# A running log-sum-exp along time: three time steps per partition instead of two, Exp written over its input, and one load split over two queues

## The chip, the cores and the metric

The kernel runs on one core of a Trainium2 chip. The metric is device time in microseconds (us). Before the change it is 1265.37 us, the median of 10 runs (1264.45 to 1265.74). The engines named below are PE (TensorE, matrix multiply), ACT (ScalarE, functions of one element), DVE (VectorE), POOL (GpSimd) and SP (SyncE, which here only issues transfers). DMA stands for the 16 engines that move data between the chip's memory and the core's buffer.

## What is computed

The input x has shape 4 x 4096 x 4128 (batch, time, feature), float32. Along time the output is the running log-sum-exp:

```python
out[:, 0, :] = x[:, 0, :]
for t in range(1, S):
    mx = np.maximum(out[:, t - 1, :], x[:, t, :])
    out[:, t, :] = mx + np.log(np.exp(out[:, t - 1, :] - mx) + np.exp(x[:, t, :] - mx))
```

The same as the logarithm of a running sum of exp(x). The kernel computes it in that form: exponential, prefix sum, logarithm. Input and output are 270.5 MB each, and each is moved once.

## The kernel before

A tile is 256 time steps of one batch: 128 partitions with R = 2 consecutive time steps each, 4128 features wide. One partition's part of a transfer is thus one run of 2 x 4128 x 4 = 33,024 bytes. There are 16 tiles per batch, 64 in all. Each is loaded into a buffer of the pool `xpool` (5 buffers), overwritten there with the result, and stored from there.

The features are cut into four chunks of 1024; the last has the 32 left-over features added. For each chunk:

- `exp` (L107, its instruction at L111) has ACT write exp(x) of both time steps, as fp16, into a buffer of a second pool, `epool` (4 buffers).
- `head` (L114) has PE add up in a PSUM buffer: a triangle of ones (`incl`) times the first time step, a strict triangle (`excl`) times the second, and `pick` times the carry. That is the running sum at each partition's first time step. There are three such PSUM buffers, used in turn. The carry of each chunk is the sum at the end of the tile before, in two fp16 parts.
- `ln(0, c)` (L125, L126) has ACT write the logarithm over x.
- `second` (L128) adds the second time step with an identity matrix, so that the buffer holds the sum at each partition's second time step.
- `close` (L133) takes the logarithm of that, and `keep` (L88) has DVE copy the last partitions into the carry with two instructions (L90, L91).

The 32 left-over features have a PSUM buffer of their own (`tail_mm`, L138) and one Ln for both time steps (L149).

The order is written out by hand (`manual_schedule`, L83), and every engine executes its instructions in that order. In `run` (L155) the chunks of one tile overlap: while chunk c is exponentiated, chunk c-1 takes its first Ln and chunk c-2 its second. At the end of a tile the chunks in flight are finished before the next tile's first Exp.

SP issues all transfers from one queue (L102 loads, L153 stores). Four loads are issued at the start; from then on the load of tile i+3 (L183) is issued ahead of tile i's work and store, and it waits until the store that last used its buffer, that of tile i-2, is done. A store waits for the last Ln of its tile, and everything behind it in SP's queue waits with it.

Of the kernel before, what the change touches and what calls it, by code (L numbers as in the profile page):

```python
# [7 lines left out]
FP32 = mybir.dt.float32  # L8
FP16 = mybir.dt.float16
ACT = mybir.ActivationFunctionType  # L10
P = 128
R = 2
CH = 1024
MM = 512
HI, LO = 96, 32
# [2 lines left out]
def _constants(nc, pool):  # L18


    def tri(base, name):
        t = pool.tile([P, P], FP16, name=name)
        nc.gpsimd.memset(t, 1.0)

        nc.gpsimd.affine_select(  # L25
            out=t, in_=t, pattern=[[1, P]], compare_op=mybir.AluOpType.is_ge,
            fill=0.0, base=base, channel_multiplier=-1,
        )
        return t

    def ones_where_zero(bases, step, name):
        t = pool.tile([P, P], FP16, name=name)
        nc.gpsimd.memset(t, 0.0)
        for base in bases:
            nc.gpsimd.affine_select(  # L35
                out=t, in_=t, pattern=[[step, P]], compare_op=mybir.AluOpType.not_equal,
                fill=1.0, base=base, channel_multiplier=1,
            )
        return t

    return (
        tri(0, "incl"),
        tri(-1, "excl"),
        ones_where_zero([0], -1, "ident"),
        ones_where_zero([-(HI + 31), -(LO + 31)], 0, "pick"),
    )


@with_exitstack
def kernel(  # L50
    ctx: ExitStack,
    tc: tile.TileContext,
    x: bass.AP,
    out: bass.AP,
):

    nc = tc.nc
    B, S, D = x.shape  # L60
    rows = P * R
    n_t = S // rows
    assert S % rows == 0
    n_main = D // CH
    tail = D - n_main * CH
    t0 = n_main * CH

    nc.scalar.preload_act_table_set("natural_log_exp_and_others")  # L68
    consts = ctx.enter_context(tc.tile_pool(name="consts", bufs=1))
    incl, excl, ident, pick = _constants(nc, consts)  # L70

    xpool = ctx.enter_context(tc.tile_pool(name="xpool", bufs=5))
    epool = ctx.enter_context(tc.tile_pool(name="epool", bufs=4))
    cpool = ctx.enter_context(tc.tile_pool(name="cpool", bufs=1))
    pmain = ctx.enter_context(tc.tile_pool(name="pmain", bufs=3, space=bass.MemoryType.PSUM))
    ptail = ctx.enter_context(tc.tile_pool(name="ptail", bufs=2, space=bass.MemoryType.PSUM))

    carry = [cpool.tile([P, CH], FP16, name=f"carry{c}") for c in range(n_main)]
    carry_t = cpool.tile([P, tail], FP16, name="carry_t")
    for t in (*carry, carry_t):  # L80
        nc.vector.memset(t, 0.0)  # L81

    ctx.enter_context(tc.manual_schedule())  # L83

    def mm(pt, w, rhs, start, stop):
        nc.tensor.matmul(pt, lhsT=w, rhs=rhs, start=start, stop=stop, skip_group_check=True)  # L86

    def keep(cr, pt):  # L88

        nc.vector.tensor_copy(cr[HI:HI + 32, :], pt[HI:HI + 32])  # L90
        nc.vector.tensor_tensor(  # L91
            out=cr[LO:LO + 32, :], in0=pt[HI:HI + 32], in1=cr[HI:HI + 32, :],
            op=mybir.AluOpType.subtract,
        )

    class Step:
        def __init__(self, b, k):
            self.first = k == 0
            self.xt = xpool.tile([P, R, D], FP32, name="xt")
            self.et, self.pt = {}, {}  # L100
            self.dram = lambda t: t[b, k * rows:(k + 1) * rows, :].rearrange("(p j) d -> p j d", j=R)
            nc.sync.dma_start(out=self.xt, in_=self.dram(x))  # L102

        def cols(self, c):
            return slice(c * CH, (c + 1) * CH if c + 1 < n_main else D)

        def exp(self, c):  # L107
            s = self.cols(c)
            w = s.stop - s.start
            et = epool.tile([P, R, CH + tail], FP16, name="et")  # L110
            nc.scalar.activation(et[:, :, :w], self.xt[:, :, s], ACT.Exp)  # L111
            self.et[c] = et

        def head(self, c):  # L114
            et = self.et[c]
            pt = self.pt[c] = pmain.tile([P, CH], FP32, name="pt")
            for s in range(0, CH, MM):
                mm(pt[:, s:s + MM], incl, et[:, 0, s:s + MM], True, False)
            for s in range(0, CH, MM):
                mm(pt[:, s:s + MM], excl, et[:, 1, s:s + MM], False, self.first)  # L120
            if not self.first:
                for s in range(0, CH, MM):
                    mm(pt[:, s:s + MM], pick, carry[c][:, s:s + MM], False, True)

        def ln(self, j, c):  # L125
            nc.scalar.activation(self.xt[:, j, c * CH:(c + 1) * CH], self.pt[c], ACT.Ln)  # L126

        def second(self, c):  # L128
            pt = self.pt[c]
            for s in range(0, CH, MM):  # L130
                mm(pt[:, s:s + MM], ident, self.et[c][:, 1, s:s + MM], False, True)

        def close(self, c):  # L133

            self.ln(1, c)
            keep(carry[c], self.pt[c])

        def tail_mm(self):  # L138
            et = self.et[n_main - 1]
            qt = self.qt = ptail.tile([P, R, tail], FP32, name="qt")  # L140
            e0, e1 = et[:, 0, CH:], et[:, 1, CH:]
            for j in range(R):
                mm(qt[:, j, :], incl, e0, j == 0, False)
                mm(qt[:, j, :], incl if j else excl, e1, False, self.first)
                if not self.first:
                    mm(qt[:, j, :], pick, carry_t, False, True)

        def ln_tail(self):
            nc.scalar.activation(self.xt[:, :, t0:D], self.qt, ACT.Ln)  # L149
            keep(carry_t, self.qt[:, 1, :])  # L150

        def store(self):
            nc.sync.dma_start(out=self.dram(out), in_=self.xt)  # L153

        def run(self):  # L155
            last = n_main - 1
            self.exp(0)
            self.head(0)
            for c in range(1, n_main):
                self.exp(c)  # L160
                self.head(c)
                if c == last:
                    self.tail_mm()
                self.ln(0, c - 1)
                self.second(c - 1)
                if c >= 2:
                    self.close(c - 2)
            self.ln(0, last)
            self.second(last)
            self.close(last - 1)  # L170
            self.ln_tail()
            self.close(last)
            self.store()

    work = [(b, k) for b in range(B) for k in range(n_t)]
    ahead = 3
    steps = []
    for i, (b, k) in enumerate(work):
        if i == 0:
            steps += [Step(*work[n]) for n in range(ahead)]  # L180
        if i + ahead < len(work):
            n = i + ahead
            steps.append(Step(*work[n]))  # L183
        steps[i].run()


# [28 lines left out]
```

The softmax here doesn't subtract the row's maximum and nothing guards it: scores larger than these inputs give would overflow.

## Time and profile before

| | |
|---|---|
| median of 10 runs | 1265.37 us |
| the profiled execution's own time | 1265.42 us |
| its span, first to last instruction | 1263.6 us |
| moved over the span | 541.5 MB, 428 GB/s to and from memory |
| ACT busy: Exp (L111) | 485.5 us in 256 instructions |
| ACT busy: Ln (L126) | 504.6 us in 512 instructions |
| DVE busy: carry (L90 and L91) | 314.8 and 314.0 us in 256 each |
| PE: 512-column matmuls | 505 ns mean with `incl` or `excl`, 427 ns with `ident` |
| loads, issue to landing | 64 of 4128 KB, median 29.4 us |
| stores, issue to landing | 64 of 4128 KB, median 38.7 us |

In a group's row, the numbers after the bar are its busy time, the mean duration of one in ns, and the idle time of the engine just ahead of it with what ended that idle time. A row of waits has who waited, for whom, and then the total in us, how often, and the longest. In a row of the timeline come the start, the time until the end of the last of the instructions merged in it, the engine and line, and how many there are.

### The profile page before, as it was taken

What the parts mean: (1) busy time and instruction counts of PE and PEld (TensorE: products, weight loads), DVE (VectorE), ACT (ScalarE), POOL (GpSimd) and SP (SyncE); (2) the same over time, 40 slices, a digit from 0 to 9 for tenths busy, and PEclk for the clock granted to TensorE, in tenths of its full rate; (3) what the DMA queues carried; (4) which work ended last, traced back from release to release, by engine and by line L of the source; (5) the groups of instructions that cost most, each with busy time, mean ns of one, the idle gap of its engine ahead of it and who ended that gap; (6) DMA issues with size and microseconds to landing.
All of it is one profiled execution on the core that took longest, in us unless ns stands there. A gap on an engine that the chain in (4) does not pass through costs nothing.

```text
span 1263.6 us, 7025 instructions
## 1 busy us (share of the span) xinstructions
PE 663.3 (52%) x2392; PEld 242.7 (19%) x2392; DVE 655.7 (52%) x645; ACT 962.9 (76%) x833; POOL 2.2 (0%) x13
## 2 busy tenths in 40 slices
PE   2565655545545565464554645546445464554651
PEld 1222222111112121121121211212112121121210
DVE  3565565464454544645546455464564544545443
ACT  6889878778778787786877877778778787787872
POOL 0000000000000000000000000000000000000000
PEclk9878878767687677877767777777777777767776
DMA  9999999999999999999999999999999999999997
GB/s 401 418 431 431 432 430 431 432 429 432 432 435 433 432 430 433 432 434 430 433 434 433 431 432 432 433 432 433 434 434 434 433 428 432 432 434 432 434 433 330
DMA packets 18466, 541.51 MB, mean 429 GB/s; under 512 B 2048, under 2 KB 2048, under 8 KB 2048
## 3 DMA queue, kind: packets, MB, share of 16 engines
q1 hardware_dynamic: 18432, 541.07, 99.5%
q8 instruction: 19, 0.31, 0.1%
q14 instruction: 15, 0.12, 0.0%
HBM read 270.53 MB, written 270.53 MB: 428 GB/s over the span
## 4 chain that ended last, share of the span: by engine, by line
DMA 81%; ACT 2%; PE 1%; SPq 1%; DVE 1%; issue 0%; ACTq 0%
DMA out_dram<-xt 77%; DMA xt<-in_x_dram 5%; ACT et L111 1%; ACT xt L126 1%; PE pt L86 1%; SPq L102 1%; DVE carry L90 0%; DVE carry L91 0%; SPq L153 0%; DVE carry_t L90 0%; DVE carry_t L91 0%; ACTq L126 0%
## 5 line engine op out<-in xcount | busy, mean ns | idle before, releaser
L90 DVE CAST carry<-pt 32x1024 f16<-32x1024 f32 x256 | 314.8, 1230 | 575.0 <-ACT xt L126 571.8
L111 ACT ACTIVATE et<-xt 128x2048 f16<-128x2048 f32 (+1 forms) x256 | 485.5, 1921 | 153.3 <-DMA xt<-in_x_dram 153.3
L126 ACT ACTIVATE xt<-pt 128x1024 f32<-128x1024 f32 x512 | 504.6, 1029 | 123.4 <-PE pt L86 62.6
L86 PE MATMUL pt<-et,incl 128*128 128x512 f16 x512 | 211.1, 505 | 548.5 <-ACT et L111 379.6
L91 DVE TENSOR_TENSOR carry<-pt,carry 32x1024 f16<-32x1024 f32 x256 | 314.0, 1226 | 8.8
L86 PE MATMUL pt<-et,excl 128*128 128x512 f16 x512 | 211.5, 505 | 0.0
L86 PEld LDWEIGHTS <-incl 128*128 128x128 f16 x704 | 69.2, 111 | 683.1 <-issue 631.6
L86 PE MATMUL pt<-carry,pick 128*128 128x512 f16 x480 | 195.2, 498 | 0.0
L86 PE MATMUL pt<-et,ident 128*128 128x512 f16 x512 | 174.5, 427 | 27.3 <-ACT xt L126 27.3
L86 PEld LDWEIGHTS <-excl 128*128 128x128 f16 x576 | 71.2, 124 | 115.8 <-issue 83.3
L86 PEld LDWEIGHTS <-pick 128*128 128x128 f16 x600 | 69.8, 119 | 94.8 <-issue 66.7
L86 PEld LDWEIGHTS <-ident 128*128 128x128 f16 x512 | 49.5, 106 | 102.1 <-issue 76.2
L86 PE MATMUL qt<-et,incl 128*128 128x32 f16 x192 | 19.6, 189 | 0.0
L86 PE MATMUL qt<-carry_t,pick 128*128 128x32 f16 x120 | 15.6, 182 | 0.0
L149 ACT ACTIVATE xt<-qt 128x64 f32<-128x64 f32 x64 | 14.5, 227 | 0.0
L90 DVE CAST carry_t<-qt 32x32 f16<-32x32 f32 x64 | 12.6, 196 | 2.0
L91 DVE TENSOR_TENSOR carry_t<-qt,carry_t 32x32 f16<-32x32 f32 x64 | 12.4, 193 | 2.2
L86 PE MATMUL qt<-et,excl 128*128 128x32 f16 x64 | 11.6, 182 | 0.0
L81 DVE MEMSET carry<- 128x512 uint32 x4 | 1.9, 485 | 1.1 <-PEq L199 1.0
L68 ACT ACT_TABLE_LOAD x1 | 1.3, 1283 | 0.8 <-PEq L199 0.8
L35 POOL TENSOR_SCALAR_AFFINE_SELECT pick<-pick 128x128 f16<-128x128 f16 x2 | 0.6, 298 | 0.1
L25 POOL TENSOR_SCALAR_AFFINE_SELECT incl<-incl 128x128 f16<-128x128 f16 x1 | 0.3, 298 | 0.0
(11 smaller groups left out, 1.9 us busy)
## 6 DMA issues: line engine op xcount, KB each, us to landing
xt<-in_x_dram SPq DMA_DIRECT2D x64, 4128.0 KB, 29.4
out_dram<-xt SPq DMA_DIRECT2D x64, 4128.0 KB, 38.7
```

The source lines that it names most:

```text
L25: nc.gpsimd.affine_select(out=t, in_=t, pattern=[[1, P]], compare_op=mybir.AluOpType.is_ge, fill=0.0, base=base, channel_multiplier=-1,)
L35: nc.gpsimd.affine_select(out=t, in_=t, pattern=[[step, P]], compare_op=mybir.AluOpType.not_equal, fill=1.0, base=base, channel_multiplier=1,)
L68: nc.scalar.preload_act_table_set("natural_log_exp_and_others")
L81: nc.vector.memset(t, 0.0)
L86: nc.tensor.matmul(pt, lhsT=w, rhs=rhs, start=start, stop=stop, skip_group_check=True)
L90: nc.vector.tensor_copy(cr[HI:HI + 32, :], pt[HI:HI + 32])
L91: nc.vector.tensor_tensor(out=cr[LO:LO + 32, :], in0=pt[HI:HI + 32], in1=cr[HI:HI + 32, :], op=mybir.AluOpType.subtract,)
L102: nc.sync.dma_start(out=self.xt, in_=self.dram(x))
L111: nc.scalar.activation(et[:, :, :w], self.xt[:, :, s], ACT.Exp)
L126: nc.scalar.activation(self.xt[:, j, c * CH:(c + 1) * CH], self.pt[c], ACT.Ln)
L149: nc.scalar.activation(self.xt[:, :, t0:D], self.qt, ACT.Ln)
```

## The change

Rows: R is 3. A tile is 384 time steps, three per partition, so that one run is 49,536 bytes. 4096 steps are 32 x 128, which makes ten tiles of three and one of two per batch, 44 tiles in all. In the first batch the tile of two comes first, in the others last.

Buffers: Exp writes fp16 into the first half of the bytes of its own x columns (a view of the same buffer as fp16). `epool` is gone; `xpool` has four buffers of three rows.

Order: the work is cut into chunks with stages. `head` adds the first time step with `incl` and all others with `excl`. `stage(j)` takes the Ln of time step j, then adds step j+1 with the identity; after the last step it keeps the carry. In each round of a tile the stages of three chunks are emitted, the oldest first, then the Exp two chunks on and the `head` one chunk on. A tile's chunks are finished before the next tile begins. The tail's matmuls read the same columns several times over by a broadcast view.

Transfers: three loads are issued at the start. After that each tile's store is issued at its end and then the load three tiles on. That load uses the buffer of the tile before, and so waits for the store before. One load, issued after the 23rd tile, is split: 80 partitions on SP, 45 on POOL, 3 on SP, with a small load into `pad` on POOL before and after.

```diff
-R = 2
+R = 3
...
-    xpool = ctx.enter_context(tc.tile_pool(name="xpool", bufs=5))
-    epool = ctx.enter_context(tc.tile_pool(name="epool", bufs=4))
+    bufs = 4
+    xpool = ctx.enter_context(tc.tile_pool(name="xpool", bufs=bufs))
...
+        def load(self, split=False):
+            full = xpool.tile([P, R, D], FP32, name="xt")
+            self.xt = full[:, :self.r, :]
+            self.half = self.xt.bitcast(FP16)
+            if not split:
+                nc.sync.dma_start(out=self.xt, in_=self.dram(x))
+                return
...
+            pad = cpool.tile([12, 16], FP32, name="pad")
+            nc.gpsimd.dma_start(out=pad[:5, :], in_=x[0, :5, :16])
+            nc.sync.dma_start(out=self.xt[:80], in_=self.dram(x)[:80])
+            nc.gpsimd.dma_start(out=self.xt[80:125], in_=self.dram(x)[80:125])
+            nc.sync.dma_start(out=self.xt[125:], in_=self.dram(x)[125:])
+            nc.gpsimd.dma_start(out=pad, in_=x[0, :12, :16])
...
+        def e(self, j, a, b):
+            return self.t.half[:, j, 2 * self.c * CH + a:2 * self.c * CH + b]
...
+        def exp(self):
+            c0, w = self.c * CH, self.w
+            nc.scalar.activation(
+                self.t.half[:, :, 2 * c0:2 * c0 + w], self.t.xt[:, :, c0:c0 + w], ACT.Exp,
+            )
...
+        def head(self):
+            t = self.t
+            pt = self.pt = pmain.tile([P, CH], FP32, name="pt")
+            for j in range(t.r):
+                for s in range(0, CH, MM):
+                    mm(pt[:, s:s + MM], excl if j else incl, self.e(j, s, s + MM), start=j == 0)
+            if not t.first:
+                for s in range(0, CH, MM):
+                    mm(pt[:, s:s + MM], pick, carry[self.c][:, s:s + MM])
+            if self.c == last:
+                self.tail_head()
...
+            for i in range(r):
+                e = self.e(i, CH, CH + tail)
+                mm(qt[:, i:, :], incl, to(e, r - i), start=i == 0)
+                if i:
+                    mm(qt[:, :i, :], excl, to(e, i))
+            if not t.first:
+                mm(qt, pick, to(carry_t, r))
...
+        def stage(self, j):
...
+            t, c, pt = self.t, self.c, self.pt
+            nc.scalar.activation(t.xt[:, j, c * CH:(c + 1) * CH], pt, ACT.Ln)
+            if j + 1 < t.r:
+                for s in range(0, CH, MM):
+                    mm(pt[:, s:s + MM], ident, self.e(j + 1, s, s + MM), stop=j + 2 == t.r)
+                if c == last and j == 0:
+                    nc.scalar.activation(t.xt[:, :, t0:D], self.qt, ACT.Ln)
+                    keep(carry_t, self.qt[:, t.r - 1, :])
+            else:
+                keep(carry[c], pt)
...
+    ahead = bufs - 1
+    for s in steps[:ahead]:
+        s.load()
+    for n, s in enumerate(steps):
+        chunks = [Chunk(s, c) for c in range(n_main)]
+        chunks[0].exp()
+        chunks[1].exp()
+        chunks[0].head()
+        for g in range(n_main + s.r - 1):
+            for d in range(s.r - 1, -1, -1):
+                if 0 <= g - d < n_main:
+                    chunks[g - d].stage(d)
+            if g + 2 < n_main:
+                chunks[g + 2].exp()
+            if g + 1 < n_main:
+                chunks[g + 1].head()
+        s.store()
+        if n + ahead < len(steps):
+            steps[n + ahead].load(split=n == len(steps) // 2)
```

## The prediction

> **What bounds the kernel now.** I read the page first: engine totals, the DMA slices, the queues, the chain that ended last.
>
> ```profile
> PE 663.3 (52%) x2392; PEld 242.7 (19%) x2392; DVE 655.7 (52%) x645; ACT 962.9 (76%) x833; POOL 2.2 (0%) x13
> ...
> DMA  9999999999999999999999999999999999999997
> ...
> DMA packets 18466, 541.51 MB, mean 429 GB/s; under 512 B 2048, under 2 KB 2048, under 8 KB 2048
> ...
> q1 hardware_dynamic: 18432, 541.07, 99.5%
> ...
> DMA 81%; ACT 2%; PE 1%; SPq 1%; DVE 1%; issue 0%; ACTq 0%
> ```
>
> One queue keeps the 16 DMA engines busy for 99.5% of the span; ACT, the busiest engine, has 76%. Then SP's waits: the load of L102 waits for an older store, that is for DMA itself, not for compute.
>
> ```profile
> SPq L102 <- DMA out_dram<-xt: 1083.8, 59, 19.5
> ```
>
> Next, stretches of the end (columns: window, length, PE, PEld, DVE, ACT, POOL, clock, DMA share, GB/s).
>
> ```profile
> 1250.00:1253.00 3.00, 0.00 (x0) 0.00 (x0) 0.00 (x0) 0.00 (x0) 0.00 (x0) 0.50 0.94 407
> 1253.00:1255.00 2.00, 0.00 (x0) 0.00 (x0) 0.00 (x0) 0.00 (x0) 0.00 (x0) 0.50 0.80 347
> 1255.00:1257.00 2.00, 0.00 (x0) 0.00 (x0) 0.00 (x0) 0.00 (x0) 0.00 (x0) 0.50 0.42 182
> 1257.00:1259.00 2.00, 0.00 (x0) 0.00 (x0) 0.00 (x0) 0.00 (x0) 0.00 (x0) 0.50 0.23 99
> 1259.00:1261.00 2.00, 0.00 (x0) 0.00 (x0) 0.00 (x0) 0.00 (x0) 0.00 (x0) 0.50 0.08 33
> ```
>
> The engines do not stop together: by 1258 under a quarter of them still work. The landing records of the last store say the same: first engine at 1253.8, fifteenth at 1261.0, last at 1262.75. So the time is the amount of transfer of the slowest engine. Last, the ACT side, since a change of its order could make it the bound: groups by shape, and one tile that did not wait for its load.
>
> ```profile
> L126 ACT ACTIVATE xt<-pt 128x1024 f32<-128x1024 f32 x512 | 504.6, 1029 | 123.4 <-PE pt L86 62.6 <-issue 59.4 <-ACT et L111 0.6
> L111 ACT ACTIVATE et<-xt 128x2048 f16<-128x2048 f32 x192 | 359.3, 1904 | 153.3 <-DMA xt<-in_x_dram 153.3
> ```
>
> ```profile
> 28.50 3.73 ACT L111 ACTIVATE et<-xt 128x2048 f16<-128x2048 f32 x2
> 33.30 1.02 ACT L126 ACTIVATE xt<-pt 128x1024 f32<-128x1024 f32 x1 [1.07 <-PE pt L86]
> ...
> 36.02 1.93 ACT L126 ACTIVATE xt<-pt 128x1024 f32<-128x1024 f32 x2
> ...
> 42.17 1.94 ACT L126 ACTIVATE xt<-pt 128x1024 f32<-128x1024 f32 x2 [0.54 <-PE pt L86]
> ...
> 45.01 3.73 ACT L111 ACTIVATE et<-xt 128x2048 f16<-128x2048 f32 x2
> ```
>
> Such a tile took 45.01 - 28.50 = 16.5 us; DMA needs 8.454 MB / 433 GB/s (steady rate in the windows) = 19.5 us for its load and store. ACT waits the rest: 153.3 us for loads. Two Ln in 1.93 us instead of 2 x 1.02 show that neighbours overlap by 0.11.
>
> [...]
>
> **The change, part by part.**
>
> Bytes: unchanged, 541 MB. Below that DMA time cannot fall, so the gain is at most what packets and unevenness cost.
>
> Longer runs. A packet of 33,024 B took 1.222 us (median of the trace's packet records), one of 8,192 B (instructions) 0.309. The line through both is 27.2 B/ns and 7.8 ns per packet[...]. A packet of 49,536 B is then 7.8 + 1821.2 = 1829 ns, not shown by the trace. One engine moves 8 packets of each transfer: before 128 x 8 = 1024 x 1.222 = 1251.3 us, and 128 semaphore packets of 9 ns, 1.2. After: 40 tiles of three rows and 4 of two, 88 loads and stores: 640 x 1.829 + 64 x 1.222 = 1248.8, and some 92 x 9 ns = 0.8. Gain 2.9 us. Bounds: 0, if a run this long is served as several packets; 320 x 13 ns = 4.2, if all of 99.5% x 16 x 1263.6 / 16,384 = 1.228 us over the 1.214 that 27.2 B/ns needs were paid per packet. I take 2.9, as two sizes lie on one line.
>
> Split load (step 25: 80 rows on SP, 45 on POOL, 3 on SP). [...] If the spared engine is the one that lands last (1262.75), the next decides, 1260.99: gain 1.8. If it is another: 0, or 1.8 lost when one of the three was last. I take 1.5 of gain. The POOL queue holds nothing else by then; SP issues two pieces, 0.33 to 0.43 us each in the timeline, where a queue of tens of us stands behind it (store to landing 38.7 us median).
>
> Exp and the pools. [...] so 3 x 2.75 + 2.83 + 12 x 1.03 (Ln) + 0.25 (tail) = 23.7 us of ACT for three rows, less 17 overlaps of 0.11: 21.9. Matmuls per row stay 4 x 512 columns and chunk half; carry copies fall from 256 to 176 pairs of 2.46 us. In-place writing removes the fp16 pool; I cost it at nothing.
>
> Drain per tile. The stalls that this order leaves on ACT: (a) at the start, Exp 0 (2.75), eight cold matmuls (0.43 each, 3.4) and their end and signal, 0.36: first Ln at 6.5, Exp 1 issued out by 5.3: 1.2. (b) The matmuls of chunk 3 need chunk 0's PSUM buffer: third Ln of chunk 0 ends at 15.7, two carry copies 2.5, signal 0.1, eight warm matmuls 8 x 0.215 + 0.3: ready 20.3, ACT free 19.2: 1.1. (c) At the end the last Ln waits for two identity matmuls, 0.8. Sum 3.1: one tile 25.0 us; with all matmuls cold the same walk gives 28.8. The DMA period of a tile is 16 x 1.829 = 29.3 us. So ACT is covered, by 4.3 us or, all cold, by 0.5. Sum over the kernel: 40 x 25 + 4 x 18 = 1072 us of ACT under 1250 of DMA.
>
> Four buffers, load behind store. Load 3 is no longer issued at once but after store 0. DMA has loads 0 to 2 until 1.8 + 9.8 + 2 x 14.7 = 41 us; store 0 is out at 13.3 (landing of load 0 now) + 18 = 31: cover 10 us. Then store 1 at 56 against 65. Later the queue holds a load and a store, 29 us, when SP waits for store n-1: no gap. At the end, load 43 landing at 0: DMA has store 41 until 14.7; tile 42's compute ends near 5.5, so store 42 follows until 29.4; tile 43 ends at 24.5. Covered too.
>
> Sum on the profiled execution: 1263.6 - 2.9 - 1.5 = 1259.2 us of span; the run around it was 1265.42, 1.8 more, and equals the median 1265.37. Forecast 1261.0.
>
> **The rivals.**
> 1. No gain: long runs cost what they did and the spared engine was not the last. 1265.4 - 0.3 (semaphores) to + 1.8: about 1265. For it: which engine is last is not in any view. Against: two packet sizes on one line. 0.15.
> 2. Slower, ACT: x, Exp and result now share a buffer that matmuls read. If each wait is taken per buffer, not per column range, every Ln stands behind the matmuls issued before it and every group of matmuls behind the Exp before it. The same walk in strict turns gives 37 us for a three-row tile, 25 for a two-row one: 13 + 40 x 37 + 4 x 25 + 10 = 1603. It decides from 29.3 us per tile, 4.3 over my walk; each us beyond costs 40. For it: nothing in this trace shows two engines on parts of one buffer at once. Against: the parts are disjoint. 0.12.
> 3. Slower, DMA: the longer run is served less well; 1% on 80 large transfers is 640 x 18 ns = 11.7 us, 1261 + 11.7 = 1273. For it: no run of that length in the trace. Against: 8 KB and 33 KB have one rate. 0.12.
> 4. More gain: the engines also drift apart less with fewer packets. The mean engine is idle for 12% of the last 63.6 us, 7.6, of which some 3 more could go: 1257. 0.05.
>
> **How the numbers follow.** Forecast 0.56, its own range 1258.5 to 1263.5 (packet cost 0 to 4.2, relief 0 to 1.8). About 0.2%, 2.5 us, is what a measurement of this kernel can tell from no change, so the line is 1262.8. Of the forecast 0.51 lies below and 0.05 within; rival 4 adds 0.05 faster, rival 1 0.02 faster and 0.13 within; rivals 2 and 3 0.24 slower. Faster 0.58, same 0.18, slower 0.24. The range runs 1257.0 to 1269.0: it takes in the forecast, rivals 1 and 4 and the lower part of 3.
>
> **What would show it.** Right: hardware queue near 99.5% again, about 11,300 large packets, GB/s 433 or 434 in the middle slices, ACT still waiting for loads (by about 29.3 - 25 = 4 us a tile), last windows that fall off more steeply. Wrong: ACT waiting for PE in every tile with SP's store waiting for ACT and DMA digits under 9 (rival 2); 433 falling with DMA digits at 9 (rival 3); a gap between 31 and 65 us (buffers); the same staircase at the end (rival 1).

## The result, and the profile after

The changed kernel takes 1288.35 us (median of 8 runs, 1286.31 to 1290.43), beside 1265.42 for the kernel before in the same comparison: ratio 1.0182, 95% interval 1.0173 to 1.0190. It is 23 us slower where 4 us of gain were forecast. The profiled execution took 1288.76 us, with a span of 1287.0.

The page of the changed kernel, first the DMA rows in 40 slices of 32.2 us, then its queues:

```profile
DMA  9999999999999999999999999999999999999997
GB/s 402 427 429 430 436 426 438 425 435 439 425 439 432 431 440 425 435 431 437 428 368 302 308 430 435 433 432 437 429 436 433 434 429 437 429 437 434 427 429 321
DMA packets 12788, 541.47 MB, mean 421 GB/s; under 512 B 1494, under 2 KB 1494, under 8 KB 1494
...
q1 hardware_dynamic: 12630, 538.84, 98.2%
q0 software_dynamic: 128, 2.23, 1.1%
```

The digit of busy DMA is 9 in all slices but the last, as before. The row under it is the one to read: three slices in the middle moved 368, 302 and 308 GB/s, and the others about what they moved before. Against 433 the three lack (65 + 131 + 125) x 32.2 / 433 = 23.9 us. The whole loss sits in one place, and there the DMA engines are busy but slow. Queue q0 is POOL's; its 128 packets are those of the split load and its two small ones, and nothing else uses it.

Windows of 10 us over that place (columns as in the prediction; the last three are PE clock, DMA share and GB/s; a packet counts whole in the window where it starts, so a share can pass 1):

```profile
660.00:670.00 10.00, 7.08 (x22) 2.64 (x22) 0.00 (x0) 9.22 (x7) 1.02 (x2) 0.75 1.26 391
670.00:680.00 10.00, 6.00 (x24) 2.15 (x23) 6.50 (x7) 6.89 (x9) 0.00 (x0) 0.83 0.91 163
680.00:690.00 10.00, 0.33 (x2) 0.00 (x0) 3.71 (x4) 1.02 (x1) 0.00 (x0) 0.60 0.94 183
690.00:700.00 10.00, 0.00 (x0) 0.10 (x1) 0.00 (x0) 1.39 (x1) 0.00 (x0) 0.50 0.92 367
700.00:710.00 10.00, 7.46 (x19) 2.60 (x19) 0.00 (x0) 8.84 (x5) 0.00 (x0) 0.53 1.07 413
710.00:720.00 10.00, 6.74 (x23) 2.40 (x22) 4.80 (x4) 8.55 (x7) 0.00 (x0) 0.83 1.00 228
720.00:730.00 10.00, 2.23 (x14) 0.77 (x12) 5.42 (x7) 4.13 (x5) 0.00 (x0) 0.82 0.92 248
```

There are two dips. The pieces of the split load are issued at 663; POOL's queue is empty, so its 45 rows start 4 us later (first packet at 667.5), while the 80 rows on SP stand behind some 40 us of earlier work: 67.6 us from issue to landing, beside 31.8 for POOL's rows. The first dip, 660 to 700, lacks (42 + 270 + 250 + 66) x 10 / 433 = 14.5 us; the second, 700 to 730, lacks 9.5. The packet records name the cause more closely: packets of 49,536 B took 1.829 us almost everywhere, but POOL's 45 took 3.5 to 6.2 us each. SP's whole transfers beside them were slow too, most of their packets at 2.9 to 5 us, and in the second dip the slow packets took mostly 3.5 to 4. PE, DVE and ACT have almost nothing to do from 690 to 698.6, because ACT waits 17.2 us for a load there.

### The profile page after: what moved, and what is told of

It reads as the page before. It is cut to its first block, busy times and chain, and to the rows that moved or that the text cites. A ratio compares the mean times of both kernels' runs of the same rounds, so it can differ in the third digit from the quotient of the medians.

```text
span 1287.0 us, 6175 instructions
## 1 busy us (share of the span) xinstructions
PE 682.8 (53%) x2268; PEld 244.0 (19%) x2268; DVE 451.4 (35%) x445; ACT 977.1 (76%) x733; POOL 3.9 (0%) x16
## 4 chain that ended last, share of the span: by engine, by line
DMA 56%; ACT 21%; PE 18%; issue 2%; another core or an unknown queue 1%; DVE 0%; ACTq 0%; SPq 0%
DMA xt<-in_x_dram 32%; DMA out_dram<-xt 24%; PE pt L87 18%; ACT xt L171 12%; ACT xt L137 9%; ACT xt L176 0%; DVE carry L91 0%; DVE carry L92 0%; PE qt L87 0%; ACTq L237 0%; ACTq L137 0%; SPq L113 0%
## 5 line engine op out<-in xcount | busy, mean ns | idle before, releaser
L137 ACT ACTIVATE xt<-xt 128x3072 f16<-128x3072 f32 (+3 forms) x176 | 475.3, 2701 | 103.6 <-DMA xt<-in_x_dram 102.2
L91 DVE CAST carry<-pt 32x1024 f16<-32x1024 f32 x176 | 216.4, 1230 | 721.6 <-ACT xt L171 716.8
L87 PE MATMUL pt<-xt,ident 128*128 128x512 f16 x672 | 235.3, 437 | 315.0 <-ACT xt L171 314.4
L87 PE MATMUL pt<-xt,incl 128*128 128x512 f16 x352 | 156.3, 539 | 269.4 <-ACT xt L137 268.9
L87 PE MATMUL pt<-xt,excl 128*128 128x512 f16 x672 | 259.7, 526 | 0.0
L92 DVE TENSOR_TENSOR carry<-pt,carry 32x1024 f16<-32x1024 f32 x176 | 215.9, 1226 | 6.1
L87 PEld LDWEIGHTS <-excl 128*128 128x128 f16 x756 | 94.5, 127 | 148.6 <-issue 120.4
L87 PE MATMUL pt<-carry,pick 128*128 128x512 f16 x320 | 119.6, 462 | 0.0
L87 PEld LDWEIGHTS <-incl 128*128 128x128 f16 x480 | 51.5, 111 | 356.3 <-issue 305.5
L87 PEld LDWEIGHTS <-pick 128*128 128x128 f16 x360 | 42.3, 117 | 64.0 <-issue 46.9
## 6 DMA issues: line engine op xcount, KB each, us to landing
xt<-in_x_dram SPq DMA_DIRECT2D x1, 3870.0 KB, 67.6
xt<-in_x_dram POOLq DMA_DIRECT2D x1, 2176.9 KB, 31.8
```

Source lines behind the costliest of these rows:

```text
L92: nc.vector.tensor_tensor(out=cr[LO:LO + 32, :], in0=pt[HI:HI + 32], in1=cr[HI:HI + 32, :], op=mybir.AluOpType.subtract,)
L137: nc.scalar.activation(self.t.half[:, :, 2 * c0:2 * c0 + w], self.t.xt[:, :, c0:c0 + w], ACT.Exp,)
```

## The experiments

Three theories stood at the start. P: the pieces themselves are slow, because each covers only some of the partitions, so that their packets take a multiple. Why they should be slow no trace or run of this case shows. Q: what costs is POOL's queue, whose transfer takes turns with SP's: in the trace of the changed kernel POOL's packets begin in three rounds of 15, at 667.5, 676.8 and 685.2, with 18 and 16 packets of SP begun between the starts of the rounds. R: the tiles of three rows, the four buffers or the drain cost, and the dip is where it shows.

**The split alone taken out.**

```diff
-            steps[n + ahead].load(split=n == len(steps) // 2)
+            steps[n + ahead].load()
```

> The changed kernel with all loads whole on SP; nothing is left out. Theory P (the split load alone costs[...]): the three slices at 302 to 368 GB/s return to 433, which is 23.9 us of transfer, so 1288.35 - 24 = about 1264; with the longer runs' 2.9 us gain at work it stands at or a little under the kernel before, 1261 to 1265. Theory R (tiles of three rows, four buffers or the drain cost): above 1275, and the dip in GB/s stays somewhere in the middle.

Measured: 1263.38 us (21 runs), ratio to the kernel before 0.9984 (0.9977 to 0.9990). The split load cost 1288.35 - 1263.38 = 25.0 us. Everything else in the change is 2.0 us of gain. The same place in this kernel:

```profile
660.00:670.00 10.00, 5.46 (x24) 2.24 (x24) 1.16 (x1) 9.94 (x8) 0.00 (x0) 1.00 1.00 433
670.00:680.00 10.00, 6.02 (x24) 2.12 (x23) 6.63 (x9) 6.80 (x9) 0.00 (x0) 0.83 1.01 436
680.00:690.00 10.00, 6.24 (x15) 2.15 (x15) 2.43 (x2) 9.07 (x5) 0.00 (x0) 0.52 0.99 428
```

No dip. R falls. This is also the version that beats both kernels.

**The split alone put into the kernel before**, in batch 2, tile 3:

```diff
-            nc.sync.dma_start(out=self.xt, in_=self.dram(x))
+            if (b, k) != (2, 3):
+                nc.sync.dma_start(out=self.xt, in_=self.dram(x))
+            else:
+                pad = cpool.tile([12, 16], FP32, name="pad")
+                nc.gpsimd.dma_start(out=pad[:5, :], in_=x[0, :5, :16])
+                nc.sync.dma_start(out=self.xt[:80], in_=self.dram(x)[:80])
+                nc.gpsimd.dma_start(out=self.xt[80:125], in_=self.dram(x)[80:125])
+                nc.sync.dma_start(out=self.xt[125:], in_=self.dram(x)[125:])
+                nc.gpsimd.dma_start(out=pad, in_=x[0, :12, :16])
```

> The kernel before, with one load in the middle (batch 2, tile 3) cut into the same pieces 80, 45 and 3 with the two small POOL loads. Theory P: the same loss on runs two thirds as long, 24 x 2/3 = 16 us, so about 1281. Theory R: the split is harmless, 1264 to 1267.

Measured: 1279.03 us, ratio 1.0107 (1.0094 to 1.0121), 13.7 us lost beside 1265.36. The loss needs neither tiles of three nor long runs. It is 55% of 25.0, where the shorter runs alone would give two thirds; that difference is not explained.

**Two pieces on SP, 80 and 48 partitions.**

```diff
-            nc.sync.dma_start(out=self.xt[:80], in_=self.dram(x)[:80])
-            nc.gpsimd.dma_start(out=self.xt[80:125], in_=self.dram(x)[80:125])
-            nc.sync.dma_start(out=self.xt[125:], in_=self.dram(x)[125:])
+            nc.sync.dma_start(out=self.xt[:80], in_=self.dram(x)[:80])
+            nc.sync.dma_start(out=self.xt[80:], in_=self.dram(x)[80:])
```

(The two `pad` loads are dropped too.)

> The changed kernel with the split load in two pieces, 80 and 48 partitions, both on SP; no POOL transfer. Theory P: [...] 1262 + 11 to 17 = 1273 to 1279. Theory Q (POOL's queue and its turns with SP's are what costs): 1261 to 1265, no dip.

Measured: 1285.02 us, 21.6 over the kernel without a split. Q does not explain it, as POOL moves nothing here. P has the sign, but its size was too small: 11 to 17 expected, and what that size rested on no trace shows. By the packet records, read in order of time, the 80 rows took about 3.7 us each, twice the normal, and most of the 48 rows 4.3 to 6.8, which is 2.4 to 3.7 times.

**Two halves of 64 on SP**, in the same place (here, in the next and in the last one the two lines shown stand in place of the three pieces, and the `pad` loads are dropped):

```diff
+            nc.sync.dma_start(out=self.xt[:64], in_=self.dram(x)[:64])
+            nc.sync.dma_start(out=self.xt[64:], in_=self.dram(x)[64:])
```

> The changed kernel with the split load in two pieces of 64 partitions, both on SP. Every DMA engine gets 4 + 4 rows, the same amount as in a whole load, so the count of packets per engine is even. Theory P: [...] the load takes 29.3 us instead of 14.6: about 1262 + 14.6 = 1277, with packets of 3.66 us. Theory Q, and the count of packets by engine that the prediction used: no loss, 1261 to 1265.

Measured: 1277.42 us, 14.0 over the kernel without a split; expected 1277.

```profile
680.00:690.00 10.00, 6.03 (x14) 2.00 (x14) 2.52 (x3) 9.10 (x5) 0.00 (x0) 0.53 1.07 403
690.00:700.00 10.00, 6.67 (x24) 2.48 (x23) 3.33 (x3) 9.41 (x9) 0.00 (x0) 0.84 1.12 233
700.00:710.00 10.00, 3.77 (x19) 1.31 (x17) 6.83 (x8) 4.43 (x6) 0.00 (x0) 0.84 0.90 188
710.00:720.00 10.00, 0.00 (x0) 0.00 (x0) 0.06 (x1) 0.00 (x0) 0.00 (x0) 0.50 0.95 277
```

Half the rate at a full DMA share: the packets of this load took mostly 3.67 to 3.9 us, twice 1.829. P's doubling came true in size; what doubles the time was not shown. The records have 1424 semaphore packets for 89 transfers, 16 each, and the slow packets come in eight rounds of up to 16. So the load is spread over the DMA engines as evenly as a whole one, in eight rounds, and still takes twice as long. Counting packets by engine, as the prediction did, gives nothing here.

**The even partitions, then the odd ones**, both on SP:

```diff
+            nc.sync.dma_start(out=self.xt[0::2], in_=self.dram(x)[0::2])
+            nc.sync.dma_start(out=self.xt[1::2], in_=self.dram(x)[1::2])
```

> The changed kernel with the split load in two pieces on SP: the 64 even partitions, then the 64 odd ones. [...] Theory P [...]: packets of 3.66 us and a loss of 14 us as with two halves, 1277. Theory P2 [...]: no loss, 1262 to 1265.

Measured: 1263.57 us, ratio 0.9986 (0.9979 to 0.9992), as without a split. Where the two halves of 64 had their dip:

```profile
690.00:700.00 10.00, 6.69 (x28) 2.56 (x28) 4.91 (x4) 8.11 (x7) 0.00 (x0) 0.83 1.01 436
700.00:710.00 10.00, 2.59 (x14) 0.87 (x12) 5.30 (x6) 7.69 (x7) 0.00 (x0) 0.80 0.98 426
```

The slowest packet between 500 and 900 took 2.4 us, as in the kernel without a split (2.3). So a piece of 64 rows is not slow by its size: it lost 14.0 us when its rows were neighbours and 0.2 when they were every second one. P, which had the loss in both cuts, was right that the pieces cost and wrong about this one; P2 came true. What makes a block of neighbours slow is not settled. Nor does the number of rows in a block tell how slow it is: packets of the 80 rows and of the halves of 64 took twice the normal, those of the 48 rows up to 3.7 times.

One rival was not tried by itself. Row p of a piece in the chip's memory always goes to partition p, so a limit on the memory's side would follow the same cuts. Two records speak against it. A whole tile of two steps reads 4.2 MB in a row at full rate (33,024 B in 1.222 us, 27.0 B/ns), while the 80 rows read 4.0 MB in a row at half of it (49,536 B in about 3.7 us). And in the run below with all pieces on SP, seven packets of 1.83 us follow each other from 709 to 722, by their times on one engine, while every other packet begun from 709 to 720 took 6.2 us or more: what is slow is not the memory as a whole.

**The split by time step**, so that each piece has all 128 partitions, one of them on POOL:

```diff
-            nc.sync.dma_start(out=self.xt[:80], in_=self.dram(x)[:80])
-            nc.gpsimd.dma_start(out=self.xt[80:125], in_=self.dram(x)[80:125])
-            nc.sync.dma_start(out=self.xt[125:], in_=self.dram(x)[125:])
+            nc.sync.dma_start(out=self.xt[:, 1:, :], in_=self.dram(x)[:, 1:, :])
+            nc.gpsimd.dma_start(out=self.xt[:, 0, :], in_=self.dram(x)[:, 0, :])
```

> The changed kernel with the split load cut by time step instead of by partition: steps 1 and 2 of all 128 partitions on SP, step 0 of all 128 on POOL, the two small POOL loads as before. Theory P [...]: every piece has 128 partitions, [...] so no loss: 1262 to 1265, like the kernel without a split, and no slice under 425 GB/s. Theory Q (POOL's ring and its turns with SP's): what the split on SP alone left unexplained, 3 us, or more, is lost here too: 1266 or above.

Measured: 1263.50 us, ratio 0.9986 (0.9979 to 0.9993). POOL's 128 packets of 16,512 B took 0.615 us at the median, the full 27 B/ns, and without the ends no slice is under 426 GB/s. POOL's queue, its two small loads and its turns with SP's queue cost nothing that can be measured when the piece has all 128 partitions (0.1 us beside the kernel without a split).

**The pieces as they are, all on SP**:

```diff
-            nc.gpsimd.dma_start(out=self.xt[80:125], in_=self.dram(x)[80:125])
+            nc.sync.dma_start(out=self.xt[80:125], in_=self.dram(x)[80:125])
```

> The changed kernel with its pieces of 80, 45 and 3 partitions as they are, but all three on SP; the two small POOL loads stay. Theory P: nearly the whole loss stays, since the pieces are the same: 1284 to 1288, beside 1285.0 for 80 and 48 on SP. Theory Q (the piece on POOL costs by overtaking what SP has queued): the POOL piece's 15 us mostly go, 1272 to 1276.

Measured: 1290.95 us, 27.6 over the kernel without a split. The loss does not go when POOL's piece moves to SP (the 2.6 us more than in the changed kernel lie within the spread of both: 1288.83 to 1291.89 beside 1286.31 to 1290.43). Q falls for these pieces.

**Half on SP, half on POOL**:

```diff
+            nc.sync.dma_start(out=self.xt[:64], in_=self.dram(x)[:64])
+            nc.gpsimd.dma_start(out=self.xt[64:], in_=self.dram(x)[64:])
```

> The changed kernel with the split load in two halves of 64 partitions, the first on SP, the second on POOL, so that both are in progress at once. Theory P: [...] the loss is under the 14 us of two halves one after the other, between 0 and 14: 1263 to 1277. Theory Q: POOL's half costs more than SP's did, above 1277.4.

Measured: 1284.60 us, 21.2 over the kernel without a split, where P had at most 14; here what Q said came true. The windows show why P's premise, both halves in progress at once, was wrong:

```profile
670.00:680.00 10.00, 6.31 (x24) 2.16 (x23) 6.53 (x8) 6.54 (x9) 0.00 (x0) 0.83 0.95 238
680.00:690.00 10.00, 0.00 (x0) 0.00 (x0) 3.10 (x3) 0.73 (x1) 0.00 (x0) 0.57 1.07 228
690.00:700.00 10.00, 0.00 (x0) 0.11 (x1) 0.00 (x0) 2.10 (x1) 0.00 (x0) 0.50 0.86 357
700.00:710.00 10.00, 7.91 (x20) 2.70 (x20) 0.00 (x0) 8.78 (x6) 0.00 (x0) 0.57 1.09 398
710.00:720.00 10.00, 6.99 (x30) 2.70 (x30) 4.91 (x4) 8.07 (x8) 0.00 (x0) 0.83 1.07 253
```

The halves were never in progress together. POOL's ran first, beside the whole transfers that SP had queued, and SP's followed in a second dip. From 660 to 700 the rate lacks 11.9 us, from 700 to 730 another 6.6, about half of what two halves on SP lost. So a half on POOL costs more than a half on SP. The packet records show where: POOL's 64 packets come in four rounds of 16, at 3.4 to 4.2 us, and between the rounds SP's whole transfers run slow as well, all 32 of their packets begun from 670 to 680 taking 2.6 to 3.5 us. A half on POOL thus slows the whole transfers that it overtakes. Why a packet of a whole transfer is slow beside it was not tried.

## Why the prediction was wrong

**The step that failed** is the split load. The prediction took "1.5 of gain", with 1.8 lost at worst, from a count of the packets that each DMA engine would move. How the rows of such pieces spread over the engines the trace of before does not show. In the trace of the changed kernel POOL's 45 packets of 49,536 B come in three rounds of 15. But the count also supposed that a packet takes 1.829 us in any piece. In these pieces it took two to more than three times that (3.5 to 6.2 us for POOL's), and the term measured 25.0 us of loss where 1.5 of gain stood. The prediction left out which partitions each piece covers. By the runs that is what decides: two halves of 64 neighbouring partitions lost 14.0 us, with packets of twice the time, the even and the odd ones 0.2. 80 and 48 rows lost 21.6. Nothing in the trace of before warned of it, since all its transfers have 128 partitions.

**What bounds the kernel**: right. Without the split 37 of the 40 slices stand at 427 to 443 GB/s, all but the first two and the last.

**The longer runs**: right. A packet of 49,536 B was worked out as 1829 ns, and 1829 is its median. The forecast gain was 2.9 us and 2.0 was measured without the split; the last engine's landing came 2.1 earlier (1260.64 beside 1262.75). The time of all the queue's packets, divided by the 16 engines, fell by 2.7 us (1256.9 to 1254.2), which bears out the working. The remaining 0.9 is not settled.

**The drain and the ACT walk**: right in kind, too small in size. Two tiles of three rows of the kernel without a split that did not wait for loads, in the timeline of ACT:

```profile
58.17 5.55 ACT L137 ACTIVATE xt<-xt 128x3072 f16<-128x3072 f32 x2
64.58 1.02 ACT L171 ACTIVATE xt<-pt 128x1024 f32<-128x1024 f32 x1 [0.86 <-PE pt L87]
...
69.81 1.02 ACT L171 ACTIVATE xt<-pt 128x1024 f32<-128x1024 f32 x1 [0.49 <-PE pt L87]
...
80.40 1.02 ACT L171 ACTIVATE xt<-pt 128x1024 f32<-128x1024 f32 x1 [1.82 <-PE qt L87]
82.10 0.25 ACT L176 ACTIVATE xt<-qt 128x96 f32<-128x96 f32 x1 [0.68 <-PE pt L87]
...
84.86 1.02 ACT L171 ACTIVATE xt<-pt 128x1024 f32<-128x1024 f32 x1 [0.68 <-PE pt L87]
85.78 5.55 ACT L137 ACTIVATE xt<-xt 128x3072 f16<-128x3072 f32 x2
...
113.17 5.55 ACT L137 ACTIVATE xt<-xt 128x3072 f16<-128x3072 f32 x2
```

A tile takes 27.6 and 27.4 us, not 25.0. The first Ln of chunk 3, at 80.40, waits 1.82 where the walk had 1.1. PE shows why:

```profile
77.31 1.06 PE L87 MATMUL pt<-xt,incl 128*128 128x512 f16 x2
78.16 1.72 PE L87 MATMUL pt<-xt,excl 128*128 128x512 f16 x4
79.72 0.60 PE L87 MATMUL pt<-carry,pick 128*128 128x512 f16 x2
80.31 0.20 PE L87 MATMUL qt<-carry_t,pick 128*128 128x96 f16 x1
```

The chunk's eight matmuls run from 77.31 to 80.32, 3.0 us where the walk had 2.0 (8 x 0.215 + 0.3): the first two take 78.16 - 77.31 = 0.85, 0.43 each. ACT's row names the tail's matmuls (`qt`), but they end only 0.2 us later. The tail's Ln waits 0.68 more, which the walk did not have. The Exp of three rows fit: 2.75 us (at 65.50) and 2.84 for the last chunk (at 70.73), where the walk had 2.75 and 2.83. All that stays under the 29.3 us of DMA, so it costs nothing, but the cover is 2 us a tile and not 4.3. ACT's wait for loads says the same: 77.3 us over 44 tiles, 1.8 a tile where 4 were forecast.

**The buffers**: right. Without the split no slice between the first two and the last is under 427 GB/s.

**The rivals.** The second (waits per buffer) did not occur: such a tile takes 27.5 us in the kernel without a split, not 37. The third had the right direction and the right thing to look for, "433 falling with DMA digits at 9", but the wrong reason: long runs go at full rate (49,536 B in 1.829 us, 27.1 B/ns), and runs of 33,024 B lose as well when the load is cut in this way. No case had a loss from the split above 1.8 us, so the chance of 0.24 for slower stood on other mechanisms.

## What to carry to other kernels

Where DMA is the bound, do not cut a transfer into blocks of neighbouring partitions without measuring it: here a cut by time step lost 0.1 us and one by every second partition 0.2, and every cut into blocks of partitions lost 14 us or more on runs of this length. Look at GB/s beside the busy share, because slow engines read as busy: a share of 0.91 to 1.00 stood beside 163 to 248 GB/s here. A balance of a few us between DMA engines is to be priced with the rate at which the pieces run, not with the count of their packets.

## What the runs showed that was not expected

One load of 6.3 MB, 1.2% of all traffic, cost 25.0 us, more than the 14.6 that such a load takes. A split in two halves cost 14.0, or 0.2, by nothing but which 64 rows are in which half. And a half cost more on the queue that was empty than on the one that was full (about 12 us beside 7).
